# Product order within a row pair, and operand offsets, in a float32r/bf16 matmul kernel

## The chip, the cores and the metric

One core of one Trainium2 chip. The metric is the device time of one launch in microseconds, on the slowest (here the only) core. Executions of one kernel agree within 0.3%, so a change of 1% can be read, but only with several runs. A ratio below is the mean time of one kernel's fast runs over that of the other's fast runs of the same rounds, so it isn't quite the ratio of the medians quoted beside it.

## The reference

```python
batch, seq, hidden = 16, 512, 768
x:     (16, 512, 768)  float32
w_qkv: (768, 2304)     float32
qkv = np.matmul(x, w_qkv)
return np.stack([q, k, v], axis=0)     # the three column blocks of qkv, float32
```

As a matrix product this is 8192 x 768 by 768 x 2304.

## The kernel before

The rows are cut into 32 pairs of 128-row blocks, p = 0 to 31. The columns are two quads of 1024 (q = 0 and 1; a and b below) and a remainder of 256. From p = 3 on, each quad is computed by a Winograd-like scheme with seven products. Products 1 and 2 take bf16 operands, products 3 to 7 take float32r sums of blocks. Each product is three matmuls of 128 x 128 by 128 x 512. The remainder is twelve bf16 matmuls of 256 columns.

```python
    def product(u, n, ps, start):
        t1, t2, t3, t4 = ts[u.q]
        if n <= 2:                       # bf16
            h = (n - 1) * KH
            lhs = [xb[u.p][:, h + j, :P] for j in range(KH)]
            rhs = [b1[u.q][:, h + j, :] for j in range(KH)]
        else:                            # float32r
            k, t = {3: (4, b22[u.q][:]), 4: (0, t4), 5: (1, t1), 6: (2, t2), 7: (3, t3)}[n]
            lhs = [sr[u.p][:, k, j, :] for j in range(KH)]
            rhs = [t[:, j, :] for j in range(KH)]
        for j in range(KH):
            nc.tensor.matmul(ps[:], lhs[j], rhs[j], ...)      # arguments cut

    def two(a, b, early):                # one pair
        do(a, 1)
        do(b, 1)
        early()                          # work of the next pair on the other engines
        do(a, 2)
        do(a, 6)
        do(b, 2)
        do(b, 6)
        do(a, 5)
        do(a, 7)
        do(b, 5)
        do(b, 7)
        do(a, 4)
        rem(a.p)
        do(b, 4)
        do(a, 3)
        store_quad(a)
        do(b, 3)
        store_quad(b)
```

A matmul has a stationary operand, which a weight load (LDWEIGHTS) brings in ahead of it, and a moving one. bf16 elements have 2 bytes, float32r elements 4; the profile calls float32r f32. The stationary operands (`lhs`) are tiles xb and s; the moving ones (`rhs`) are b1, w_rem, b22, t_0 (quad a) and t_1 (quad b). The pools are laid out in the order of their creation. The pool "w" comes first, with w_rem, b1, b22 and t_0, all multiples of 512 bytes, and at its end two small tiles: `tiny`, 4 bytes that take 32, and `eye`, 256. Then come tq (which holds t_1) and, further on, xb and s. Modulo 512 bytes the addresses are 128 for w_rem, b1, b22 and t_0, and 416 for t_1, xb and s.

## Time and profile before

| | before |
|---|---|
| time, median | 367.14 us (366.92 to 367.59) |
| TensorE busy | 98% of the span |
| granted clock | 0.997 |
| one looped pair, 54 matmuls | 10.873 us |
| looped pairs | 28, so 304 us of the 365 |

How to read it: TensorE is the chain, at full clock and without waits. What can still change is the distance from one matmul's start to the next.

### The profile page before, as it was taken

The numbers are of one execution on the slowest core, as the hardware profiler recorded it, in microseconds if no ns is written. First come the engines' busy times: TensorE is split into PE (matmuls) and PEld (weight loads), VectorE is DVE, ScalarE is ACT, GpSimd is POOL, SyncE is SP. The second block draws the span as 40 slices with busy tenths as digits, with TensorE's granted clock in tenths as the row PEclk, the third lists the DMA queues.
The fourth block names the chain that finished last, engine by engine and source line by source line (L and its number), as shares of the span: only waits on it lengthen the run. The fifth ranks groups of instructions, "written<-read, shape, count | busy, mean of one in ns | idle before, by whom it ended". The sixth has DMA issues, their size and how long they took to land.

```text
span 364.8 us, 5274 instructions
## 1 busy us (share of the span) xinstructions
PE 358.0 (98%) x1797; PEld 243.8 (67%) x1797; DVE 225.8 (62%) x239; ACT 182.4 (50%) x304; POOL 173.7 (48%) x180
## 2 busy tenths in 40 slices
PE   7999999999999999999999999999999999999995
PEld 3544576666776666776666777676777676777663
DVE  3589746765557665557666556666556766556732
ACT  4557554454454454554455544545545444445442
POOL 0000961655665445665444665444665544566410
PEclk9999999999999999999999999999999999999998
DMA  7999979988899899999888899888899989899767
GB/s 297 382 375 336 347 245 335 327 284 293 273 313 311 264 285 296 277 301 321 278 274 289 281 300 318 284 271 284 288 297 310 296 258 292 291 286 316 261 251 267
DMA packets 80617, 108.08 MB, mean 296 GB/s; under 512 B 4816, under 2 KB 60368, under 8 KB 80592
## 3 DMA queue, kind: packets, MB, share of 16 engines
q1 hardware_dynamic: 65184, 96.35, 80.8%
q10 hardware_dynamic: 15408, 11.41, 9.9%
q8 instruction: 14, 0.23, 0.3%
q14 instruction: 11, 0.09, 0.1%
HBM read 32.24 MB, written 75.50 MB: 295 GB/s over the span
## 4 chain that ended last, share of the span: by engine, by line
PE 97%; DMA 1%; ACT 1%; DVE 0%; issue 0%
PE ps L206 76%; PE ps L256 12%; PE ps L381 9%; DMA xin<-in_x_dram 1%; PE ps L161 1%; ACT xc L141 0%; ACT xb L141 0%; DVE xb L139 0%; ACT orem L311 0%
## 5 line engine op out<-in xcount | busy, mean ns | idle before, releaser
L206 PE MATMUL ps<-t,s 128*128 128x512 f32 x696 | 188.0, 412 | 0.0
L206 PEld LDWEIGHTS ps<-t,s 128*128 128x128 f32 x696 | 128.7, 188 | 30.9
L169 POOL CAST xb<-xf 128x1536 bf16<-128x1536 f32 x29 | 43.9, 1514 | 171.6 <-DVE xf L124 160.1
L124 DVE STREAM_TRANSPOSE xf<-xin 128x1536 f32<-128x1536 f32 x29 | 86.8, 2991 | 6.8 <-DMA xin<-in_x_dram 3.9
L206 PE MATMUL ps<-b,xb 128*128 128x512 bf16 x348 | 85.2, 381 | 0.0
L240 DVE TENSOR_TENSOR o<-o,ps 128x512 f32<-128x512 f32 x58 | 39.9, 688 | 59.3 <-PE ps L206 59.2
L234 DVE TENSOR_TENSOR o<-o,ps 128x512 f32<-128x512 f32 x58 | 39.8, 687 | 54.1 <-ACT o L233 54.1
L206 PEld LDWEIGHTS <-xb 128*128 128x128 bf16 x348 | 29.4, 98 | 42.8 <-issue 14.7
L233 ACT ACTIVATE o<-ps 128x512 f32<-128x512 f32 x58 | 34.8, 600 | 45.2 <-PE ps L206 45.2
L220 ACT ACTIVATE o<-ps 128x512 f32<-128x512 f32 x58 | 34.7, 599 | 43.3 <-DVE o L240 34.6
L227 ACT ACTIVATE o<-ps 128x512 f32<-128x512 f32 x58 | 34.8, 600 | 41.9 <-PE ps L206 41.9
L256 PE MATMUL ps<-w_rem,xb 128*128 128x256 bf16 x384 | 47.5, 273 | 0.0
L206 PE MATMUL ps<-b,s 128*128 128x512 f32 x174 | 44.9, 393 | 0.0
L256 PEld LDWEIGHTS <-xb 128*128 128x128 bf16 x384 | 35.0, 98 | 12.4 <-issue 8.1
L224 DVE TENSOR_TENSOR o<-o,ps 128x512 f32<-128x512 f32 x58 | 36.5, 669 | 2.3 <-ACT o L220 1.3
L206 PEld LDWEIGHTS ps<-b,s 128*128 128x128 f32 x174 | 32.7, 188 | 7.7
L237 ACT ACTIVATE o<-ps 128x512 f32<-128x512 f32 x58 | 34.7, 598 | 4.5 <-ACT orem L311 0.4
L178 POOL TENSOR_TENSOR s<-s,xf 128x384 fp32r<-128x384 f32 x29 | 30.1, 1038 | 2.3
L177 POOL TENSOR_TENSOR s<-xf 128x384 fp32r<-128x384 f32 x29 | 30.9, 1066 | 0.0
L266 ACT ACTIVATE orem<-ps 128x512 f32<-128x512 f32 x31 | 18.6, 599 | 23.5 <-PE ps L256 23.5
L181 POOL TENSOR_TENSOR s<-xf,s 128x384 fp32r<-128x384 f32 x29 | 29.5, 1019 | 0.0
L179 POOL TENSOR_TENSOR s<-xf 128x384 fp32r<-128x384 f32 x29 | 29.2, 1006 | 0.0
(36 smaller groups left out, 128.1 us busy)
## 6 DMA issues: line engine op xcount, KB each, us to landing
out_dram<-o SPq DMA_DIRECT2D x62, 768.0 KB, 5.2
out_dram<-o SPq DMA_DIRECT2D x65, 256.0 KB, 4.8
xin<-in_x_dram SPq DMA_DIRECT2D x62, 192.0 KB, 6.8
xin<-in_x_dram ACTq DMA_DIRECT2D x54, 192.0 KB, 5.6
out_dram<-orem SPq DMA_DIRECT2D x31, 256.0 KB, 2.3
st<-in_w_qkv_dram SPq DMA_DIRECT2D x6, 768.0 KB, 14.1
xin<-in_x_dram SPq DMA_DIRECT2D x3, 768.0 KB, 5.8
st<-in_w_qkv_dram SPq DMA_DIRECT2D x6, 256.0 KB, 6.2
```

Of the source, the lines that this page charges most:

```text
L124: nc.vector.transpose(t[:].rearrange("p j (g b) -> p g j b", b=G), xin.pop(p)[:].rearrange("p g (a j) -> p g j a", a=G),)
L169: nc.gpsimd.tensor_copy(out=xb[p][:], in_=xf[p][:])
L206: nc.tensor.matmul(ps[:], lhs[j], rhs[j], start=(start and j == 0), stop=(j == KH - 1), skip_group_check=True,)
L220: nc.scalar.activation(c11, u.x[:], ident)
L224: nc.vector.tensor_tensor(c11, c11, u.z[:], op=add)
L227: nc.scalar.activation(c12, u.x[:], ident)
L233: nc.scalar.activation(c22, u.x[:], ident)
L234: nc.vector.tensor_tensor(c22, c22, u.y[:], op=add)
L237: nc.scalar.activation(c21, u.x[:], ident)
L240: nc.vector.tensor_tensor(c12, c12, u.y[:], op=add)
L256: nc.tensor.matmul(ps, xb[p][:, j, r * P:(r + 1) * P], w_rem[:, j, :], start=(j == 0), stop=(j == KT - 1), skip_group_check=True,)
L381: nc.tensor.matmul(ps[n][:], xb[p][:, j, r * P:(r + 1) * P], w[:, j, :], start=(j == 0), stop=(j == KT - 1), skip_group_check=True,)
```

## The change

The intent: change between bf16 and float32r as seldom as can be, and give the two operands of every matmul one offset modulo 512 bytes.

```diff
-                nc.tensor.transpose(ps[:, j, :], cols[:, j, :], eye[:])
+                nc.tensor.transpose(ps[:, j, :], cols[:, j, :], eye)
...
         do(a, 2)
+        do(b, 2)
+        rem(a.p)
         do(a, 6)
-        do(b, 2)
         do(b, 6)
         ...
         do(a, 4)
-        rem(a.p)
-        do(b, 4)
         do(a, 3)
         store_quad(a)
+        do(b, 4)
         do(b, 3)
...
-    eye = w_pool.tile([P, P], bf16, name="eye")
+    eye = w_pool.tile([P, 240], bf16, name="eye")[:, :P]
```

## The prediction

> **What bounds the kernel now.** I read the page from the top: busy time, slices, the chain that ended last, then the groups of instructions.
>
> ```profile
> span 364.8 us, 5274 instructions
> PE 358.0 (98%) x1797; PEld 243.8 (67%) x1797; DVE 225.8 (62%) x239; ACT 182.4 (50%) x304; POOL 173.7 (48%) x180
> ...
> PEclk9999999999999999999999999999999999999998
> DMA  7999979988899899999888899888899989899767
> ...
> PE 97%; DMA 1%; ACT 1%; DVE 0%; issue 0%
> ```
>
> TensorE is busy for 98% of the span at the full clock, and the chain of work that ended last is TensorE for 97% of its length. So a wait that is removed on another engine is worth nothing. DMA at 8 to 9 tenths is the only other thing that is nearly full. What can change the time is the pace at which one matmul follows another.
>
> ```profile
> L206 PE MATMUL ps<-t,s 128*128 128x512 f32 x696 | 188.0, 412 | 0.0
> L206 PEld LDWEIGHTS ps<-t,s 128*128 128x128 f32 x696 | 128.7, 188 | 30.9
> L206 PE MATMUL ps<-b,xb 128*128 128x512 bf16 x348 | 85.2, 381 | 0.0
> L206 PEld LDWEIGHTS <-xb 128*128 128x128 bf16 x348 | 29.4, 98 | 42.8 <-issue 14.7
> L256 PE MATMUL ps<-w_rem,xb 128*128 128x256 bf16 x384 | 47.5, 273 | 0.0
> ```
>
> The mean ns of a matmul (412, 381) is its latency: successive ones overlap, so it is not the pace. The last column says that the matmuls never waited (0.0). The weight loads did, with "issue" as the reason. The pace comes from the order of time:
>
> ```profile
> 150.07 1.48 PE L256 MATMUL ps<-w_rem,xb 128*128 128x256 bf16 x12
> 151.31 0.94 PE L206 MATMUL ps<-t,s 128*128 128x512 f32 x3
> 152.09 1.55 PE L206 MATMUL ps<-b,s 128*128 128x512 f32 x6
> 153.48 2.12 PE L206 MATMUL ps<-b,xb 128*128 128x512 bf16 x9
> ...
> 156.61 4.49 PE L206 MATMUL ps<-t,s 128*128 128x512 f32 x18
> 160.94 1.48 PE L256 MATMUL ps<-w_rem,xb 128*128 128x256 bf16 x12
> ```
>
> The same group comes back after 160.94 - 150.07 = 10.87 us. This is one row pair p, with 54 matmuls: 12 bf16 products of 512 columns, 12 bf16 remainder products of 256, 30 float32r of 512. The loop makes 28 of them through two() and one through last(). The start stamps in the trace are very steady (all 28 pairs take 10.866 to 10.874 us), so I averaged each start-to-start distance over the 28 pairs. I write a for the quad q=0, b for q=1, and the product's number, three matmuls each:
>
> - bf16 after bf16: 215.9 ns (512 columns), 109.2 ns (256).
> - float32r, products b5 and b7: 226.7 ns from the second matmul on.
> - float32r, a5, a7, a4, a3, b3: 229 to 235 ns, mean 232.
> - The first bf16 after a float32r takes 226 instead of 216, or 120 instead of 109: 10.5 ns more.
> - From the last bf16 over the first float32r: 447.5 ns (a6), 445.0 (b6), 342.5 (b4), against 442.6, 442.6 and 335.9 for the two paces added: 2.4 to 6.6 ns more. The next two are at 229 to 238, so the pace settles only after some three matmuls.
>
> **What the Trainium skill says.** "TensorE: Matmul & The Clock Gate", section "Back-to-back issue gap", gives N/2.4 + 2.5 ns as the warm isolated gap, 215.8 ns at 512 columns and 109.2 at 256. The bf16 matmuls here match this to 0.1 ns, so the bf16 side has nothing left to give. Its lower figure for a sustained stream (131 ns at 512) is not seen here. The same page, section "Weight-path perf modes", says that fast weight load is on for 128 weights of a type other than FP32; the trace agrees with 98 ns against 188 ns. The same page, "Step-by-step: what each phase is for", says that loading the next weights "doesn't steal SBUF read bandwidth from the running matmul". The trace seems to disagree by some 5 ns: a5/a7 and b5/b7 have the same stationary tile s, shape and types and differ in the moving tile alone. I know of no section that gives a rule of 512 bytes for matmul operands.
>
> **The change, part by part.** Nothing is added or removed; the 1797 matmuls stay.
>
> Part 1, the offsets. The addresses of the kernel before are, modulo 512: 128 for w_rem, b1, b22 and t_0; 416 for tq (so t_1), xb and s. All these tiles are multiples of 512 bytes; the shift of 288 comes from tiny (32) and eye (256), which stand between. With eye 480 bytes wide the shift is 512, and all come to 128. So a float32r product has both operands at one offset today only in b4, b5, b6, b7 (t_1 with s). Just there the trace has the 226.7 ns pace, and products with t_0 (a4 to a7) or b22 (a3, b3) don't have it. That is a control inside the kernel before. I take it that all float32r come to 226.7.
>
> Excess over 226.7, summed from the distances: a5+a7 1394.1 - 1360.2 = 33.9 ns; a4 20.7; a3+b3 32.3; together 86.9. A few ns of these are boundary cost (the last float32r before a bf16 is at 231.6).
>
> Part 2, the order. Now float32r follows bf16 three times in a pair (a6, b6, b4) and bf16 follows float32r three times (a1, b2, rem). After it, once each. Excess of the pieces with such a boundary: a2+a6 18.2, b2+b6 21.3, rem+b4 30.4, a1 10.4 ns; b5's first 4.0. With the 86.9 this is 171 ns, which is all of 10,873 minus the ideal 12 x 215.9 + 12 x 109.2 + 30 x 226.7 = 10,702.
>
> After it one boundary of each kind stays: first bf16 10.4, last float32r before it some 5, and settling after rem some 18 (b4 has 6.6 + 4.1 + 9.2 today, the last partly due to what follows). That is an estimate of 33 ns, so a pair of 10,735 ns, 138 less than now. 28 x 0.138 = 3.87 us. In last(), which keeps its order, alignment alone gives some 0.09. The start, bf16 at 216 already, gives nothing. Sum: 3.96 us; 367.14 - 3.96 = 363.2 us, 1.1% faster. Some 2.5 us of it is alignment, 1.4 us is order.
>
> **Waits that could take their place.** In the new order a7 comes six matmuls after a6, where it was nine, and must wait for ScalarE to read the bank. The kernel before already has that distance from a7 to a4: the last a7 matmul starts at 158.64, ScalarE reads from 159.08 to 159.68, a4 starts at 160.24. So 0.56 us are spare, and the other six-matmul distances (b7 to b4) have the same. Product a3 must wait for VectorE's addition of a7: it ends at 160.40, 1.76 us after the last a7 matmul starts; a3 will start ten matmuls after, 2.27 us. 0.5 us spare. The float32r products start 1.3 us later than before, so GpSimd's sums have more time, not less. The banks rotate by eight with seven taken per pair; I followed each to its last reader, and the nearest is nine matmuls back.
>
> **Rivals.**
> 1. The boundaries cost what the weight loads show. Ahead of the first bf16 weight load the timeline has an idle stretch:
>
> ```profile
> 153.48 1.62 PEld L206 LDWEIGHTS <-xb 128*128 128x128 bf16 x9 [0.27 <-issue]
> 155.22 0.64 PEld L206 LDWEIGHTS ps<-t,s 128*128 128x128 f32 x3
> 156.13 0.33 PEld L206 LDWEIGHTS <-xb 128*128 128x128 bf16 x3 [0.27 <-issue]
> ```
>
> Two fewer per pair, 56 x 0.27 = 15 us, would be 4%: 352 us. Against it: the matmul's own start distance at these places is only 10 ns longer, and the whole excess over the ideal is 171 ns per pair, 4.8 us. I don't believe it.
>
> 2. The offset has nothing to do with the pace; t_0 is slower for another cause, such as other engines' traffic at that time. Then only the order pays: two boundaries of some 15 to 25 ns, 28 x 0.03 to 0.05 = 0.8 to 1.4 us, so 366 us. For it: b6 and b4, which have equal offsets, are at 229 to 236. Against it: they directly follow bf16, and b5 to b7 drop to 226.7 and a4 is back at 234 at once.
>
> 3. The stores become the bound. DMA moves 296 GB/s at 8 to 9 tenths; 1% faster needs 299. Stores of o land in a median of 5.2 us, and each of the five o buffers comes back after 2.5 pairs, 27 us. I think it is hidden; if not, 365 to 368 us.
>
> 4. A new wait on ScalarE or VectorE in the new order: at 0.1 us per pair it costs 2.8 us and eats most of the gain, 366 us. The spare times above speak against it.
>
> **Range and chances.** 363.2 is the working. The floor is no boundary and no excess: 367.14 - 28 x 0.171 - 0.1 = 362.2. If only one part works, it is 364.6 to 366. So 362.4 to 365.4 for 8 in 10. Over 2% faster needs 359.8, below the floor: 2 in 100. Over 2% slower needs a new wait of 0.26 us in each pair: 2 in 100.
>
> **What would show it.** Right: a pair of some 10.73 us in the recurrence of the remainder group; float32r start distances of 227 for t_0 and b22 as well; one bf16 weight load with 0.27 us of "issue" per pair, not three; no idle time before matmuls. Wrong: t_0 products still at 232 (the offset falls); distances over 300 ns in the midst of float32r products (a bank wait); PE idle with DMA as the releaser. The weakest step is the settling after rem, sized from b4 alone.

## The result, and the profile after

The changed kernel takes **363.36 us** (median of 5 runs, 363.23 to 363.80) against 367.14: ratio 0.9899, 95% interval 0.9885 to 0.9912. That is within 2%, and 0.16 us from the predicted 363.2.

The top of the page, and the group of the products with t_0 and t_1:

```profile
span 362.0 us, 5220 instructions
PE 353.5 (98%) x1765; PEld 248.6 (69%) x1797; DVE 224.4 (62%) x239; ACT 182.5 (50%) x304; POOL 174.1 (48%) x180
...
PE 96%; ACT 1%; issue 1%; ACTq 0%; DVE 0%
...
L206 PE MATMUL ps<-t,s 128*128 128x512 f32 x696 | 171.4, 395 | 0.0
```

Still 98% TensorE, and no wait of these matmuls (the 0.0 in the last column). Two traps. The trace lacks 32 of 1797 matmul records (x1765), so PE's busy time isn't to be compared between the two kernels. The weight loads are all there, one per matmul, and a load starts right after the matmul before it has started; so from here on I take distances between the starts of weight loads. And the mean of one matmul fell from 412 to 395 ns mostly for a reason of recording: a float32r matmul that follows a bf16 one is recorded some 190 ns longer than its fellows (85 behind the remainder), and there are fewer such ones now.

Who waited with "issue" as the reason, before:

```profile
PEld L206 <- issue: 14.7, 54, 0.3
PEld L256 <- issue: 8.1, 30, 0.3
```

and after (total us, times, longest us):

```profile
PEld L206 <- issue: 7.3, 28, 0.3
PEld L256 <- issue: 0.5, 2, 0.3
```

These are the changes from float32r to bf16: 84 before, 30 after. The 15.0 us that vanish from these rows are four times what the kernel gained, which was 3.8. Idle time of the weight loads is mostly beside the running matmul.

Weight loads in order of time, after (start, us, then the group):

```profile
155.22 1.41 PEld L256 LDWEIGHTS <-xb 128*128 128x128 bf16 x12
156.64 4.65 PEld L206 LDWEIGHTS ps<-t,s 128*128 128x128 f32 x21
161.33 0.64 PEld L206 LDWEIGHTS ps<-b,s 128*128 128x128 f32 x3
162.01 0.64 PEld L206 LDWEIGHTS ps<-t,s 128*128 128x128 f32 x3
162.69 0.64 PEld L206 LDWEIGHTS ps<-b,s 128*128 128x128 f32 x3
163.59 2.27 PEld L206 LDWEIGHTS <-xb 128*128 128x128 bf16 x12 [0.26 <-issue]
165.99 1.41 PEld L256 LDWEIGHTS <-xb 128*128 128x128 bf16 x12
```

The remainder comes back after 165.99 - 155.22 = 10.77 us (10.760 in the mean), against 10.873 before. Products a3, b4 and b3 start 0.68 us apart, 227 ns per matmul, for t_1 and b22 alike. Averaged over 25 pairs the distances after the remainder are, in ns, for a6, b6, a5, a7 in turn:

```
110.0 231.5 229.4 | 234.1 235.0 225.0 | 230.0 235.9 228.1 | 232.5 231.5 227.0 | 226.4 226.6 227.0 ...
```

So the even pace of 226.7 ns comes only after ten slow distances, and then holds to the end of the float32r matmuls. I call these slow distances the settling.

Once there is a small wait that the waits view doesn't list. In the second looped pair a3's first weight load starts 0.10 us late, at 64.56 us: VectorE's addition of a7, which stands behind a transpose, ends at 64.44. The matmul itself starts only some 3 ns late, but the even pace is lost, and five slow distances follow (236, 236, 228, 232, 232). That pair takes 10,794 ns, 34 more than the later ones.

The sum: the 28 looped pairs run from 44.65 to 349.20 us in the trace before and from 45.12 to 346.51 in the one after: 304.55 against 301.40, 3.15 us less. The last pair, to the end of its last matmul, gives 0.07. Some 0.3 us more lies outside the span, and I have no cause for it: time less span is 2.1 us in the runs of the old order and 1.8 us in those of the new one. The spans of the two profiled runs differ by 2.8 us only, because the loop began 0.47 us later in the one after; over the fourteen traces it begins at 44.6 to 45.4 us, so I don't put this down to the change.

### The profile page after: what moved, and what is told of

It reads as the page before. It is cut to its first block, busy times and chain, and to the rows that moved or that the text cites. A ratio compares the mean times of both kernels' runs of the same rounds, so it can differ in the third digit from the quotient of the medians.

```text
span 362.0 us, 5220 instructions
## 1 busy us (share of the span) xinstructions
PE 353.5 (98%) x1765; PEld 248.6 (69%) x1797; DVE 224.4 (62%) x239; ACT 182.5 (50%) x304; POOL 174.1 (48%) x180
## 4 chain that ended last, share of the span: by engine, by line
PE 96%; ACT 1%; issue 1%; ACTq 0%; DVE 0%
PE ps L206 75%; PE ps L256 11%; PE ps L382 9%; PE ps L362 1%; PE ps L161 1%; ACT o L237 0%; ACTq L297 0%; ACT xb L141 0%; ACT orem L311 0%; DVE xb L139 0%; ACT xc L141 0%; ACTq L313 0%; DVE zero L340 0%; ACTq L311 0%
## 5 line engine op out<-in xcount | busy, mean ns | idle before, releaser
L206 PE MATMUL ps<-t,s 128*128 128x512 f32 x696 | 171.4, 395 | 0.0
L124 DVE STREAM_TRANSPOSE xf<-xin 128x1536 f32<-128x1536 f32 x29 | 85.5, 2950 | 5.7 <-DMA xin<-in_x_dram 2.9
L206 PE MATMUL ps<-b,xb 128*128 128x512 bf16 x320 | 74.2, 379 | 1.9
L206 PEld LDWEIGHTS <-xb 128*128 128x128 bf16 x348 | 31.7, 98 | 41.6 <-issue 7.3
L206 PE MATMUL ps<-b,s 128*128 128x512 f32 x174 | 48.7, 389 | 0.0
L256 PEld LDWEIGHTS <-xb 128*128 128x128 bf16 x384 | 37.4, 98 | 11.2 <-issue 0.5
```

What stands on the lines that cost most here:

```text
L124: nc.vector.transpose(t[:].rearrange("p j (g b) -> p g j b", b=G), xin.pop(p)[:].rearrange("p g (a j) -> p g j a", a=G),)
L206: nc.tensor.matmul(ps[:], lhs[j], rhs[j], start=(start and j == 0), stop=(j == KH - 1), skip_group_check=True,)
L256: nc.tensor.matmul(ps, xb[p][:, j, r * P:(r + 1) * P], w_rem[:, j, :], start=(j == 0), stop=(j == KT - 1), skip_group_check=True,)
```

## The experiments

All twelve kernels were correct. They ran in four batches, on different chips, and each batch has its own runs of the kernel before. "Offset" means s, the stationary float32r tile, less its moving partner.

**Theory at the start:** two independent gains, alignment 2.5 us and order 1.4 us. **Rival,** from the ten slow distances above: the even pace must be settled into, and every change from bf16 to float32r throws it off, so each part needs the other.

### 1. The order alone

```diff
-    eye = w_pool.tile([P, 240], bf16, name="eye")[:, :P]
+    eye = w_pool.tile([P, P], bf16, name="eye")[:, :P]
```

(against the changed kernel)

> The new order with eye 128 columns wide again, so tq, xb and s stand 288 bytes (modulo 512) off w_rem, b1, b22 and t_0. Theory of the prediction (two independent parts): the order gives 1.4 us of its own, 365.7 us, ratio 0.996. Rival (the parts need each other: the changed kernel's trace shows the even pace of 226.7 ns only from some ten float32r matmuls after the bf16 ones, and only where the offsets are equal): about 28 ns per pair, 0.8 us, ratio 0.998, with t_0 and b22 products at 229 to 235 ns throughout.

Measured: 367.04 us against 366.94 for before, ratio 1.0005 (0.9993 to 1.0018); a pair takes 10,887 ns, 13 more than before. The order alone gains nothing. The trace:

```profile
157.55 4.72 PEld L206 LDWEIGHTS ps<-t,s 128*128 128x128 f32 x21
162.32 0.65 PEld L206 LDWEIGHTS ps<-b,s 128*128 128x128 f32 x3
163.01 0.65 PEld L206 LDWEIGHTS ps<-t,s 128*128 128x128 f32 x3
163.72 0.65 PEld L206 LDWEIGHTS ps<-b,s 128*128 128x128 f32 x3
```

The last products are 0.70 us apart, 233 ns per matmul. And b5 and b7, whose operands do have one offset here, no longer settle: 234.2, 230.0, 235.8, 228.4, 232.5, 231.6 ns, where the kernel before had 234.1, 231.6, then 226.7 four times. That alone loses 20 ns per pair. The last five are the row with which the settling after the remainder ends in run 2 as well, and the distance that follows, into a4, is 226.6: the pace is reached just when the equal offsets end. Equal offsets allow the even pace; they don't ensure it. Both theories had expected a gain; the rival was nearer.

### 2. The alignment alone

The kernel before with `eye` 240 wide.

```diff
-    eye = w_pool.tile([P, P], bf16, name="eye")
+    eye = w_pool.tile([P, 240], bf16, name="eye")[:, :P]
```

> The old order with eye 240 wide, so all operand tiles at one offset. Theory of independent parts: 87 ns per pair, 2.5 us, ratio 0.993. Rival (settling takes some ten matmuls, worth 47 ns, after each of the three boundaries to float32r, runs of 3, 18 and 9 matmuls): excess 144 ns per pair against 171 before, so only 27 ns per pair, 0.8 us, ratio 0.998; a pace of 226.7 only late in the run of 18.

Measured: 365.20 us, ratio 0.9953 (0.9941 to 0.9966); a pair takes 10,807 ns, 67 less than before. That is between the two expectations (87 and 27). After b2 the float32r run settles after three slow distances (231.6, 232.6, 231.7, then 226.7), after the remainder after six (238.4, 230.0, 235.8, 228.4, 232.5, 231.6), which is most of b4, a3, b3. So the settling is neither three matmuls always, as I had predicted, nor ten always, as the rival had it. Together:

| pair, ns | offsets as before | all at one offset |
|---|---|---|
| old order | 10,873 | 10,807 |
| new order | 10,887 | 10,760 |

Alignment is worth 67 ns in the old order and 127 in the new one; order is worth -13 without alignment and 47 with it. The parts are not independent.

### 3. One offset changed back: s alone by 288

The changed kernel with a pad ahead of the pool of s. The edit of all runs that move s, with n = 288 here:

```diff
+    pad_pool = ctx.enter_context(tc.tile_pool(name="pad", bufs=1))
     s_pool = ctx.enter_context(tc.tile_pool(name="s", bufs=2))
...
+    pad = pad_pool.tile([P, n // 2], bf16, name="pad")
+    nc.vector.memset(pad[:, :1], 0.0)
```

> The changed kernel with 288 bytes ahead of the s pool alone: s is 288 off all its partners, t_1 too; order and all else as changed. If the relative offset of stationary and moving tile sets the float32r pace: no product reaches 226.7 ns, mean near 232, a pair of about 10.88 us, ratio to before about 1.001. If t_0 and b22 are slow for another cause than the offset to s, or the offset of other tiles matters: as the changed kernel, ratio 0.990.

Measured: 367.50 us, ratio 1.0016 (1.0003 to 1.003), 10,907 ns per pair: the whole gain is gone, as the offset theory said. The float32r distances stay at 232.5 and 234.2 to the end:

```profile
162.37 0.66 PEld L207 LDWEIGHTS ps<-b,s 128*128 128x128 f32 x3
163.07 0.66 PEld L207 LDWEIGHTS ps<-t,s 128*128 128x128 f32 x3
163.77 0.66 PEld L207 LDWEIGHTS ps<-b,s 128*128 128x128 f32 x3
```

These products are 0.70 us apart, where the changed kernel had 0.68. The pad moves s against xb too; that this isn't the cause is shown by the kernel before, where s and xb have one offset and the products of t_0 are slow all the same. bf16 doesn't mind: it keeps 215.8 ns in run 1 too, where xb is off b1 by 288.

### 4. What comes ahead of float32r

```diff
     def two(a, b, early):
+        rem(a.p)
         do(a, 1)
...
         do(b, 2)
-        rem(a.p)
```

> The changed kernel with rem(a.p) as the first work of a pair, so that float32r follows a 512-column bf16 matmul and not a 256-column one. If settling takes its ten matmuls whatever came before: same as the changed kernel, ratio 0.990. If it is the entry from the short matmuls that sets it off (in the kernel before the entry from 256 columns cost 6.6 ns, from 512 2.4 to 4.9): settling shrinks, up to 46 ns per pair, 1.3 us, ratio down to 0.986.

Measured: 364.42 us, ratio 0.9933: worse than the changed kernel as a whole, but its pairs take 10,740 ns, 20 less. Seven slow distances instead of ten. The loss happened once, in the second pair. Its matmuls and the transpose on VectorE in the trace:

```profile
65.85 0.93 PE L206 MATMUL ps<-b,s 128*128 128x512 f32 x3 [1.40 <-DVE o L234]
```

```profile
60.89 3.05 DVE L124 STREAM_TRANSPOSE xf<-xin 128x1536 f32<-128x1536 f32 x1 [4.41 <-DMA xin<-in_x_dram]
```

Product a3 waits for a VectorE addition, which stands behind a transpose that waited 4.41 us for its input, right after the start phase. That pair took 12,387 ns, 1.65 us more than the others, in the profiled run; the time says the same (1.06 us more than the changed kernel, with 0.5 us gained in the pairs).

### 5. The place itself

The changed kernel with 288 bytes ahead of all tiles:

```diff
+    front = w_pool.tile([P, 144], bf16, name="front")
+    nc.vector.memset(front[:, :1], 0.0)
     w_rem = w_pool.tile([P, KT, REM], bf16, name="w_rem")
```

> The changed kernel with 288 bytes ahead of every tile, so that all operand tiles are at 416 modulo 512 and not at 128. If only the offset of the two operands to each other matters: a pair stays at 10.76 us with 226.7 ns from some ten matmuls after the remainder. If the place itself matters (128 is good, 416 is not): over 10.80 us.

Measured: 10,760 ns per pair, with the same ten slow distances to within 1 ns. So it is the offset of the operands to each other that counts; at the two places tried, 128 and 416, the place itself makes no difference.

### 6. A small offset

s by 64 bytes (the edit of run 3 with n = 64).

> The changed kernel with s alone moved by 64 bytes. If any unequal offset keeps the float32r pace at 229 to 235 ns, as the 288 of the earlier run did: a pair of 10.87 to 10.91 us. If a small shift is harmless: 10.76 us.

Measured: 10,920 ns, the slowest of all. Every distance but the first two, up to the last before bf16, is 233.0 to 233.8. A small shift is not harmless, and there is no settling here: this pace is even from the start, and slow.

### 7. The remainder first, from the third looped pair on

```diff
     def two(a, b, early):
+        if a.p >= NS + 2:
+            rem(a.p)
         do(a, 1)
...
-        rem(a.p)
+        if a.p < NS + 2:
+            rem(a.p)
```

> The remainder first from the third looped pair on; in the first two it stays behind b2. The run with the remainder first throughout had pairs of 10,740 ns against the changed kernel's 10,760, and lost 1.65 us once, in its second pair, to a late input. If that wait was all that made it slower: 26 x 20 ns = 0.5 us faster than the changed kernel, 362.8 us, ratio 0.9885. If the wait comes back in a later pair: 364.4, ratio 0.993.

Measured: **362.75 us** (362.66 to 363.22), ratio 0.9876 (0.9860 to 0.9893) against before; pairs of 10,740 ns from the third on. The second pair, still in the order of the changed kernel, took 11,046 ns in the profiled run: a3's first weight load came 0.39 us late and its matmul 0.28, behind the same addition on VectorE; that is a larger case of the wait in the changed kernel's second pair. The time is 0.6 us under the changed kernel by the medians, in another batch of runs, and 26 x 20 ns = 0.52 us was expected of it. The intervals of the two ratios overlap; what supports the gain is that the pair times within a trace vary by less than 1 ns and that all four runs here lie below all five of the changed kernel, though the slowest of the four does so by 0.01 us only. It is the fastest.

### 8. The quads swapped

```diff
-            two(quad(p, 0), quad(p, 1), early)
+            two(quad(p, 1), quad(p, 0), early)
```

> The changed kernel with the two quads of a pair swapped, so that float32r starts with the product of t_1 (b6) and not of t_0 (a6). In the run with alignment alone, b6 after bf16 settled in 4 matmuls, a6 after the remainder took 11. If the tile that starts the float32r run sets how long settling takes: up to 30 ns per pair less, 0.8 us, ratio 0.988. If it doesn't: 10.76 us per pair, ratio 0.990.

Measured: 363.47 us, ratio 0.9899, 10,760 ns per pair, with the same row of distances within 1 ns though the first tile is now t_1. My guess fell: the moving tile that starts the run doesn't set the settling. (The expectation compares two kernels: b6 after bf16 in run 2 with a6 after the remainder in the changed kernel.) Run 4 shows that other work ahead of the run changes it. The last work ahead isn't enough to tell, though: after the remainder, run 2 settled in six distances and the changed kernel in ten.

### 9 to 11. The period of the offset

s by 32, by 256, and by 448 (the last with eye and tiny moved behind s, to make room).

```diff
-    eye = w_pool.tile([P, 240], bf16, name="eye")[:, :P]
+    eye = tail_pool.tile([P, P], bf16, name="eye")[:, :]
```

(run 11 only; tiny likewise, and tail_pool is created after s_pool)

> The changed kernel with s alone moved by 32 bytes; 64 gave 233.1 to 233.8 ns at every float32r matmul and a pair of 10,920 ns. If any unequal offset costs the same: about 10,900 ns. If the cost grows with the distance from 0: between 10,760 and 10,920.

> The changed kernel with s alone moved by 256 bytes, half of 512. If the pace repeats every 512 bytes, as the change's intent says: slow, 229 to 235 ns, a pair of about 10.9 us. If it repeats every 256 bytes or less: the changed kernel's 10,760.

> The changed kernel with s 64 bytes below its partners, modulo 512 (448 above); eye and tiny stand behind s to make room, which keeps the others at one offset. If equal offsets are the one good place: slow, 10.88 to 10.92 us per pair. If a stationary tile somewhat below the moving one is as good or settles sooner[...]: 10.71 to 10.76 us.

### 12. Just below zero

Run 7 with s by 224, which is 32 below its partners modulo 256.

> The run with the late remainder-first order (pairs of 10,740 ns, 362.75 us, ratio 0.9876), with s alone moved by 224 bytes, 32 below its partners modulo 256. So far, modulo 256: 0 gives 226.7 ns after some ten slow matmuls, 32 and 64 give 233 ns, 192 gives 228.9 ns from the first matmul on. If the good places go on from 192 to 0 and the settling shortens with the distance below: 10.70 to 10.74 us per pair, ratio down to 0.9845. If 0 is the one best place: over 10.76 us, ratio 0.9890 or more.

The four with the others of their kind:

| offset | modulo 256 | pair, ns | float32r distances late in the run, ns |
|---|---|---|---|
| 0 (changed kernel, run 5) | 0 | 10,760 | 226.4 to 227.0 |
| 256 (run 10) | 0 | 10,760 | 226.2 to 227.0 |
| 32 (run 9) | 32 | 10,907 | 232.5, 234.1 |
| 288 (run 3) | 32 | 10,907 | 232.5, 234.2 |
| 64 (run 6) | 64 | 10,920 | 233.0 to 233.8 |
| 448 (run 11) | 192 | 10,787 | 225.0, 230.0, 231.7 in turn |
| 224 (run 12, order of run 7) | 224 | 10,907 | 232.8 to 233.8 |

Run 10 in the trace, 0.68 us from product to product as in the changed kernel, where run 3 had 0.70:

```profile
161.01 0.64 PEld L207 LDWEIGHTS ps<-b,s 128*128 128x128 f32 x3
161.69 0.64 PEld L207 LDWEIGHTS ps<-t,s 128*128 128x128 f32 x3
162.37 0.64 PEld L207 LDWEIGHTS ps<-b,s 128*128 128x128 f32 x3
```

Offsets 0 and 256 give the same row of distances, and so do 32 and 288. So **the pattern repeats every 256 bytes, not only every 512.** It does not repeat every 128, since 64 and 192 differ by 133 ns per pair. Run 11 in the trace:

```profile
156.74 4.65 PEld L208 LDWEIGHTS ps<-t,s 128*128 128x128 f32 x21
161.42 0.65 PEld L208 LDWEIGHTS ps<-b,s 128*128 128x128 f32 x3
162.11 0.65 PEld L208 LDWEIGHTS ps<-t,s 128*128 128x128 f32 x3
162.80 0.19 PEld L208 LDWEIGHTS ps<-b,s 128*128 128x128 f32 x1
```

161.42 to 162.80 is 1.38 us for six matmuls, 229 to 230 ns each, and the trio of distances is there from the first product on. A pace that needs no settling but is 2.2 ns longer loses to one that settles, 10,787 against 10,760, because the run of 30 is long. I had hoped that 224 would join the two virtues; with 367.42 us (ratio 1.0016) it has neither. Its pairs take 10,902 and 10,912 ns in turn.

## Why the prediction was right or wrong

The time was right (363.36 for 363.2), and so were the bound and its way: next to no wait, the gain nearly all in the start distances of float32r matmuls and their borders with bf16. That it came within 0.16 us was luck: two errors offset each other, and one step was wrong in kind.

- **"I take it that all float32r come to 226.7."** Right as the pace that is reached, wrong for the first ten. The control inside the kernel before was read rightly for t_0 against t_1 (run 3 takes the pace away by the offset alone), but it also showed b4 and b6 at 229 to 236 with equal offsets. I put that down to three matmuls of settling.
- **"Settling after rem some 18"** is the term that was mis-sized. Measured: the ten distances sum to 2,313.0 ns, 46.0 over 10 x 226.7. The other border terms (10.4 and some 5) came to 10,760 - 10,702 - 46 - 1 = 11 (the 1 is the first distance, 110.0 for 109.2). So 58 ns of excess stay and not 33, and a pair saves 113 ns and not 138: 0.7 us less over 28 pairs. The prediction had named this its weakest step.
- **What made up for it:** the pairs and the last one give 3.22 us by the traces, against the predicted 3.96. The medians give 3.78. Of the 0.56 us between, 0.3 lie outside the span, which I didn't foresee and can't explain; the rest is within the scatter of the runs (the kernel before has medians of 366.89 to 367.34 in the batches).
- **"Some 2.5 us of it is alignment, 1.4 us is order."** Wrong in kind. Alone, alignment gained 1.7 us by the medians (run 2) and order nothing (run 1). A sum of excesses, each ascribed to one part, takes for granted that the other excesses stay where they are; but alignment was worth 67 ns in one order and 127 in the other, so what a border costs depends on the offsets.
- **The rivals.** The boundaries at 0.27 us each: refuted, 15.0 us less of "issue" gave 3.8 us. The offset as an accident: refuted by run 3. Stores as the bound: no matmul waited for them. A new wait in the new order: it came, but once per run, in the second looped pair, where the transpose is late. It cost that pair 34 ns in the changed kernel, and 1.65 us in run 4. It is the wait that I had checked (a3 on VectorE's addition); the 0.5 us to spare was real but held only in the even part of the loop.

What stays open: what the settling is. Its length (3 to 10 distances in the even part of the loop) changes with the order of the work, not with the place of the tiles (run 5) nor with which tile comes first (run 8). Nor is it set by the order alone: in the first looped pair, with the same 24 bf16 matmuls ahead, there are 7 slow distances in the trace of the changed kernel, 10 in run 5, 4 in run 10 and 1 in run 8, while from the third pair on all four have ten. Many settlings end in the same row (some 230, 236, 228, 232 and 232 ns: changed kernel, runs 1, 2 and 4) and differ in what comes before it. No run shows the cause of this, nor why 192 gives a trio of distances.

## What to carry to other kernels

When matmuls run back to back with no waits, average the start distances by position in the loop: here they were steady to below 1 ns and showed 171 ns per pair that no busy share or wait shows. For float32r matmuls like the ones here, try one offset modulo 256 bytes for the stationary and moving tiles, and look for small tiles allocated between them that shift it. Then keep the float32r matmuls in one long run: here the order paid only with the alignment (47 ns against -13), and the alignment paid about twice as much with the order (127 against 67). Test the parts of a change alone before crediting each with its share.

## What the Trainium skill lacked or had wrong

- "TensorE: Matmul & The Clock Gate", section "Step-by-step: what each phase is for", says that loading the next weights doesn't steal SBUF read bandwidth from the running matmul. The runs don't show the reads. They show that for float32r the pace still depends on where the stationary tile lies against the moving one: 226.7 ns at offset 0, once settled, and 233.0 to 233.8 at 64 (run 6). No page that I read gives a rule for the offset of two matmul operands to each other; the runs show a period of 256 bytes.
- The same page, section "Back-to-back issue gap", gives one pace for all types. bf16 meets N/2.4 + 2.5 (215.8 ns at 512 columns, 215.9 measured); float32r does not get under a mean of 226.7 ns over a long run. The section's 131 ns for a sustained stream at 512 columns was not seen in any run.
- The same page, section "LDWEIGHTS (loading the stationary operand)", gives P/1.2, so 107 ns for 128 columns as an estimate from that page, and that section doesn't tell the types apart. Measured: 98 ns for bf16, 188 ns for float32r.
- No page that I read gives a cost for changing between bf16 and float32r. With offsets equal, two fewer changes of each direction per pair were worth 47 ns (run 2 against the changed kernel), some 23 ns for a change there and back, settling included.
